# Memory-token projections set between the levels of a gated recurrence, with its value and gate rows loaded earlier

## The chip, the core and the metric

One core of one Trainium2 chip runs the whole program. The metric is the device time of the kernel in microseconds (us); the median of three runs of the kernel before is 934.94 us (934.83 to 937.43). TensorE (PE) multiplies matrices, VectorE (DVE) and ScalarE (ACT) work element by element, GpSimd (POOL) issues gathers and scatters, and SyncE (SP) issues most DMAs, in the order in which they stand in its queue. TensorE's clock has two levels, 1.2 and 2.4 GHz; the profile shows what was granted as a share of 2.4 GHz (0.50 or 1.00, or a mean over a stretch).

## The reference, cut to what matters

One decoder layer is computed for 512 prompt tokens and 8 sample tokens with the same weights. Two independent parts of it meet in this change.

```
# gated linear attention (4 heads, 64 x 128 state), exact form of S_t = diag(a_t) S_(t-1) + k_t^T v_t, o_t = q_t S_t
b    = cumsum(log_a)                                   # per chunk
attn = einsum('bhid,bhjd,bhijd->bhij', q, k, exp(b_i - b_j)), causal
o    = attn @ v + (q * exp(b)) @ S
S    = exp(b_last) * S + (k * exp(b_last - b))^T @ v
o    = rms_norm(o, gla_norm_g) * silu(r)               # r: the gate rows

# memory tokens: keys and values of 256 tokens, which nothing but the cross-attention needs
mem_k, mem_v = mem @ w_mk, mem @ w_mv                  # 256 x 1024 times 1024 x 1024, twice

# then
h = layer_norm(ALPHA * h + concat(gla_o, mla_o) @ w_out)
h = layer_norm(ALPHA * h + cross_attention(h, mem_k, mem_v))
h = layer_norm(ALPHA * h + mixture_of_experts(h))      # 32 experts, 100 MB of weights
```

## The kernel before

The program is written as streams: Python generators such as `recurrence`, `memory`, `step`, `sample`, `first`. A small planner (`Streams.run`, lines 257 to 270) keeps an estimated time of TensorE, `PE.now`, and estimated times of the other engines; each `yield x` says that the stream wants to go on when `PE.now` has reached `x` (or when a condition holds). The stream of the highest priority that is due runs next, so a yield decides what lands between two pieces of a stream. The order of the matmuls on TensorE is then exactly the order in which the planner ran the streams. The instructions of the other engines and the DMAs of SP are put in order by the framework and stand near the matmuls they belong to.

`recurrence` (line 1055) has the third priority, `step` (the 8 sample tokens' gated state, line 1252) the seventh, `sample` (their later layers, line 1445) the eighth, `memory` (line 962) the eleventh. Memory work therefore comes only where all of those wait.

The attention matrix of the recurrence is built in levels. `level(lv)` (line 1109) makes, for a block size of 128, 64, 32, 16, 8, 4, 2 and 1 tokens, one tile of decayed keys and queries: a subtraction on DVE, exponentials on ACT, four products on DVE. The levels 16 to 1 and the diagonal are the fine levels, the loop `for n in range(6)` at line 1168: each is 64 small matmuls (32 x 32 outputs, two PSUM banks of the tag `psm`), and each bank is then merged into `fine` by DVE with a mask (line 1188). Three tiles serve all levels in turn, so level 2 can be built only when the matmuls of level 16 are done, and level 1 after those of level 8.

After the fine levels come the value rows `vN` and the chunk states (lines 1205 to 1228), then the gate rows `rN` (lines 1229 to 1234), then for each of four token tiles the outputs, 8 matmuls of 128 x 128 or fewer, and the gate (lines 1235 to 1248). Value and gate rows were projected long before and put aside in DRAM (`zv`, `zr`); they come back by SP. The yields `due` (line 1210) and `came[t]` (line 1234) leave 5 us of the planner's time between a load and its use.

`memory` runs 16 groups of 24 matmuls (128 x 256 outputs, `psd<-arena_r`), two for each pair of weight blocks of 512 KB: it loads a block, ACT casts it to a high part, DVE subtracts to make a low part (`load_split`, line 373), TensorE multiplies, ACT copies the result out, and the keys are transposed and put aside as `zmk`, the values as `zmv`. `first` then runs the output projection `w_out` (16 groups of two times 12 matmuls, of which 12 read `arena_c`); it starts when `recurrence` and `attention` are done. Cross-attention follows, then the experts, whose weights `in_we` come in 192 blocks of 512 KB into whatever room the arenas have.

All instructions are recorded by helpers: a matmul is line 218, a transpose 222, an operation of DVE, ACT or POOL 199, a DMA of SP 238. Tiles of the arenas share one name, `arena_f`. An f32 matmul leaves two records in the trace, an `arena_r` matmul one.

Of the kernel before, what the change touches and what calls it, by code (L numbers as in the profile page):

```python
# [36 lines left out]
LEVELS = (16, 8, 4, 2, 1)  # L37
# [260 lines left out]
def tile_hybrid_decoder_step(ctx: ExitStack, tc: tile.TileContext, a):  # L298
    nc = tc.nc
    PE = Tensor(tc, nc.tensor)  # L300
    Q = Loads(PE, nc.sync)
# [35 lines left out]
    AF_ = Arena(fpool.tile([128, COLS_F], F32, name="arena_f"), COLS_F)  # L337
# [10 lines left out]
    def after(*names):  # L348
        return lambda: done.issuperset(names)

    def room(arena, *shape, **kw):
        got = []

        def there():
            v = arena.alloc(*shape, **kw)
            if v is not None:
                got.append(v)
            return v is not None
        if not there():
            yield there  # L360
        return got[0]
# [693 lines left out]
    def recurrence():  # L1055
# [86 lines left out]
        m[16] = level(16)  # L1142
        yield ready[64]
        for c in range(2):
# [8 lines left out]
        m[8] = level(8)  # L1153
        yield ready[32]
        for c in range(2):
# [9 lines left out]
            for g in (0, 2):  # L1165
                S.copy(A[32 * g:32 * g + 32, 8 * c:8 * c + 8, 32 * g + 32:32 * g + 64], pv[32 * g:32 * g + 32])
        m[4] = level(4)
        for n in range(6):
            if n:
                kk_ = qq_ = m[LEVELS[n - 1]]  # L1170
                yield ready[LEVELS[n - 1]]
            else:
                kk_, qq_ = kT, qT
            for c in range(2):
                ps = pm()
# [28 lines left out]
        done.add("fine")  # L1204
        yield after(*(("v", t) for t in range(4)))
        vN, rN = [], []
        for t in range(4):
            vN.append((yield from room(AF_, 512)))
            Q.dma_start(vN[t], zv[:, t * 512:t * 512 + 512])
        due = PE.now + 5.0  # L1210
        St = yield from room(AF_, 4, 2, 128)
        yield due
        pk = (pd(), pd())
# [14 lines left out]
        AF_.free(kd)  # L1228
        came = []
        for t in range(4):  # L1230
            yield after(("r", t))
            rN.append((yield from room(AF_, 512)))
            Q.dma_start(rN[t], zr[:, t * 512:t * 512 + 512])
            came.append(PE.now + 5.0)
        for t in range(4):
            on = yield from room(AF_, 512)
            yield came[t]
            pss = (pd(), pd()) if t % 2 else (pm(), pm())
# [987 lines left out]
```

## Time and profile before

| what | value |
|---|---|
| median of 3 runs | 934.94 us |
| the profiled execution's own time | 936.53 us |
| span of that execution, first to last instruction | 934.8 us |
| TensorE busy | 825.0 us, 88% |
| mean granted clock | 0.919 |
| VectorE, ScalarE, GpSimd busy | 485.1, 289.1, 85.0 us |
| mean DMA rate | 247 GB/s, 230.43 MB |

The program goes through stages that follow each other on TensorE: projections and attention to about 270 us, the levels of the recurrence to about 314 us, the states and outputs of the recurrence among memory projections to about 395 us, the output projection, the cross-attention to about 569 us, its output projection, and the experts from about 640 us. A share over the whole span therefore says little; the answers below are for single stretches. "Idle" is time in which an engine had no instruction of its own running; the name after the arrow is what ended it.

### The profile page before, as it was taken

How to read it: one execution, taken by the hardware profiler on the slowest of the kernel's cores; microseconds unless marked ns; L12 is line 12 of the kernel's file. 1: busy time of each engine (PE TensorE's matmuls, PEld its weight loads, DVE VectorE, ACT ScalarE, POOL GpSimd, SP SyncE). 2: the span in 40 equal slices, each digit the busy share in tenths (PEclk: the TensorE clock that was granted, in tenths of full speed). 3: DMA queues.
4: the chain of work that ended last, by engine and by line, in shares of the span. 5: the costliest groups of instructions: out<-in, count | busy, mean ns of one | idle time of the engine just before them, and what ended most of it. 6: DMA issues, size and time to landing. Idle time of an engine off the chain costs nothing. (4 is left out here: it accounts for less than half of the span.)

```text
span 934.8 us, 17185 instructions
## 1 busy us (share of the span) xinstructions
PE 825.0 (88%) x6767; PEld 585.0 (63%) x6767; DVE 485.1 (52%) x1079; ACT 289.1 (31%) x612; POOL 85.0 (9%) x88
## 2 busy tenths in 40 slices
PE   7999999989987899999899999995899959379991
PEld 6898566667875779989588757993344334133441
DVE  5564257683756525644762264567543644253734
ACT  4322334452542144412333241112123213122421
POOL 3100111011420000000000000001200200200101
PEclk9998999999985679999899999996989979779996
DMA  7922687667771447987847664257899999969930
GB/s 252 312 71 73 188 276 230 222 224 219 247 283 49 126 151 217 350 318 278 306 169 253 216 214 154 90 183 258 326 372 408 410 407 408 409 231 408 410 119 23
DMA packets 83961, 230.43 MB, mean 247 GB/s; under 512 B 12483, under 2 KB 32989, under 8 KB 83493
## 3 DMA queue, kind: packets, MB, share of 16 engines
q1 hardware_dynamic: 74660, 203.98, 61.2%
q0 software_dynamic: 9216, 25.31, 7.7%
q8 instruction: 55, 0.90, 0.4%
q14 instruction: 30, 0.24, 0.1%
HBM read 223.11 MB, written 14.39 MB: 254 GB/s over the span
## 5 line engine op out<-in xcount | busy, mean ns | idle before, releaser
L218 PE MATMUL psd<-arena_r 128*128 128x256 f32 (+1 forms) x2208 | 294.8, 293 | 9.5 <-ACT arena_r L199 5.4
L218 PEld LDWEIGHTS psd<-arena_r 128*128 128x128 f32 x2208 | 281.2, 198 | 24.0 <-issue 12.6
L218 PE MATMUL psx<-arena_f 96*32 96x256 f32 (+1 forms) x752 | 134.0, 491 | 2.0 <-DMA arena_f<-in_latT 2.0
L199 DVE TENSOR_TENSOR arena_r<-arena_f,arena_r 128x1024 fp32r<-128x1024 f32 (+3 forms) x71 | 82.4, 1166 | 100.9 <-ACT arena_r L199 90.3
L199 ACT CAST arena_r<-arena_f 128x1024 fp32r<-128x1024 f32 (+3 forms) x73 | 71.1, 977 | 130.3 <-PE psd L218 85.5
L218 PE MATMUL psm<-arena_f 64*32 64x32 f32 (+10 forms) x1394 | 94.6, 306 | 16.1 <-DVE arena_f L199 5.7
L218 PE MATMUL pss<-arena_f 128*8 128x256 f32 (+5 forms) x478 | 85.6, 465 | 0.7 <-ACT arena_f L199 0.7
L218 PEld LDWEIGHTS psx<-arena_f 96*32 96x32 f32 (+1 forms) x752 | 44.8, 124 | 63.6 <-issue 51.9
L218 PEld LDWEIGHTS psm<-arena_f 64*32 64x32 f32 (+6 forms) x1384 | 53.4, 145 | 49.0 <-issue 28.7
L222 PE MATMUL psm<-cst,arena_f 128*128 128x128 f32 (+2 forms) x393 | 64.0, 295 | 18.2 <-ACT arena_f L199 5.1
L199 DVE TENSOR_TENSOR arena_f<-arena_f 128x1024 f32<-128x1024 f32 (+6 forms) x72 | 57.1, 827 | 37.8 <-DMA arena_f<-h2d,arena_s 33.3
L222 PEld LDWEIGHTS psm<-cst,arena_f 128*128 128x128 f32 (+2 forms) x393 | 47.6, 156 | 41.8 <-issue 18.4
L637 POOL DMA_INDIRECT arena_f<-in_latN,ixn x32 | 34.0, 1063 | 192.1 <-PE psm L218 176.9
L199 DVE SCALAR_TENSOR_TENSOR arena_f<-arena_f,psd 128x256 f32<-128x256 f32 (+2 forms) x60 | 28.8, 488 | 41.6 <-PE psd L218 32.1
L1843 POOL DMA_INDIRECT arena_f<-h2d,arena_s x24 | 24.8, 1035 | 238.6 <-PE psm L222 139.3
L218 PEld LDWEIGHTS pss<-arena_f 128*8 128x8 f32 (+3 forms) x468 | 28.0, 120 | 24.8 <-issue 14.7
L199 DVE SCALAR_TENSOR_TENSOR arena_m<-pss,arena_s,arena_m 128x512 fp32r<-128x512 f32 x32 | 24.0, 749 | 31.7 <-ACT arena_m L199 31.7
L218 PE MATMUL psx<-arena_l,arena_f 128*64 128x512 f32 x100 | 39.9, 592 | 0.0
L222 PE MATMUL pss<-cst,arena_f 128*128 128x128 f32 x32 | 7.7, 326 | 36.1 <-DVE arena_m L199 25.8
L199 DVE TENSOR_TENSOR arena_f<-arena_f,psx 128x256 f32<-128x256 f32 x16 | 6.7, 417 | 61.0 <-ACT arena_f L199 61.0
L199 ACT ACTIVATE arena_f<-psd 128x256 f32<-128x256 f32 (+3 forms) x55 | 19.9, 363 | 53.6 <-PE psd L218 43.8
L199 ACT ACTIVATE arena_f<-psx 128x256 f32<-128x256 f32 x16 | 6.1, 384 | 97.1 <-PE psx L218 91.9
(210 smaller groups left out, 945.7 us busy)
## 6 DMA issues: line engine op xcount, KB each, us to landing
arena_f<-in_we SPq DMA_DIRECT2D x129, 512.0 KB
arena_l<-in_we SPq DMA_DIRECT2D x40, 512.0 KB
arena_f<-in_latT SPq DMA_DIRECT2D x128, 144.0 KB
arena_d<-in_we SPq DMA_DIRECT2D x23, 512.0 KB
arena_f<-in_wout SPq DMA_DIRECT2D x16, 512.0 KB
arena_f<-in_memKT SPq DMA_DIRECT2D x16, 512.0 KB
arena_f<-in_wxq SPq DMA_DIRECT2D x16, 512.0 KB
arena_f<-in_memV SPq DMA_DIRECT2D x16, 512.0 KB
```

Source lines behind the costliest of these rows:

```text
L199: return f(out, *args, **kw)
L218: return self.queue(self.eng.matmul(out, lhsT, rhs, **kw))
L222: return self.queue(self.eng.transpose(out, src, ident))
L637: G.indirect_dma_start(out=out, out_offset=None, in_=src, in_offset=bass.IndirectOffsetOnAxis(ap=ix, axis=0))
L1843: G.indirect_dma_start(out=out, out_offset=None, in_=h2d, in_offset=bass.IndirectOffsetOnAxis(ap=ix, axis=0), bounds_check=NT - 1, oob_is_ ...
```

## The change

Four things change, all in `recurrence`. Ahead of level 64, of level 32 and of each fine level the yield now asks for 1 us of the planner's time beyond `PE.now` (or for the level's readiness, if later), so that a stream of lower priority gets a turn there. The loads of the four value tiles and the four gate tiles are issued together, in front of the fine levels, once both have been projected. The yields of 5 us between these loads and their use are gone; 0.5 us stand in their place, and one yield until DVE and ACT are nearly through. Nothing that is computed changes, and no instruction is added but by the planner's different order.

```
@@ -1140,7 +1140,7 @@
         m[16] = level(16)
-        yield ready[64]
+        yield max(ready[64], PE.now + 1.0)
@@ -1151,7 +1151,7 @@
         m[8] = level(8)
-        yield ready[32]
+        yield max(ready[32], PE.now + 1.0)
@@ -1165,12 +1165,20 @@
         m[4] = level(4)
+        yield after(*((z, t) for z in "vr" for t in range(4)))
+        vN, rN = [], []
+        for z, vs in ((zv, vN), (zr, rN)):
+            for t in range(4):
+                vs.append((yield from room(AF_, 512)))
+                Q.dma_start(vs[t], z[:, t * 512:t * 512 + 512])
         for n in range(6):
             if n:
                 kk_ = qq_ = m[LEVELS[n - 1]]
-                yield ready[LEVELS[n - 1]]
+                yield max(ready[LEVELS[n - 1]], PE.now + 1.0)
             else:
                 kk_, qq_ = kT, qT
+                yield PE.now + 1.0
@@ -1202,14 +1210,8 @@
         done.add("fine")
-        yield after(*(("v", t) for t in range(4)))
-        vN, rN = [], []
-        for t in range(4):
-            vN.append((yield from room(AF_, 512)))
-            Q.dma_start(vN[t], zv[:, t * 512:t * 512 + 512])
-        due = PE.now + 5.0
         St = yield from room(AF_, 4, 2, 128)
-        yield due
+        yield PE.now + 0.5
         pk = (pd(), pd())
@@ -1226,15 +1228,10 @@
         AF_.free(kd)
-        came = []
-        for t in range(4):
-            yield after(("r", t))
-            rN.append((yield from room(AF_, 512)))
-            Q.dma_start(rN[t], zr[:, t * 512:t * 512 + 512])
-            came.append(PE.now + 5.0)
+        yield PE.ready() - 0.5
         for t in range(4):
             on = yield from room(AF_, 512)
-            yield came[t]
+            yield PE.now + 0.5
```

On TensorE, from the sample tokens' state matmuls (64x256) to the chunk states (64x128), the kernel before has these rows in this order; 32x32 are the levels (32 matmuls of level 32, then six fine levels of 64), 32x256 is paged attention, `arena_r` 128x256 is a memory projection:

```order
L218 MATMUL psm<-arena_f 64x256 x8
L218 MATMUL psm<-arena_f 32x32 x96
L218 MATMUL psm<-arena_f 32x256 x16
L218 MATMUL psm<-arena_f 32x32 x128
L222 MATMUL psm<-cst,arena_f 128x128 x2
L218 MATMUL psm<-arena_f 32x32 x192
L218 MATMUL psm<-arena_f 64x256 x8
L218 MATMUL psd<-arena_r 128x256 x48
L218 MATMUL psd<-arena_f 64x128 x16
```

The changed kernel has, from the same place (the first 32x32 row is level 32), and up to the third fine level:

```order
L218 MATMUL psm<-arena_f 32x32 x32
L218 MATMUL psm<-arena_f 32x256 x16
L218 MATMUL psm<-arena_f 64x256 x8
L222 MATMUL psm<-cst,arena_f 128x128 x2
L218 MATMUL psd<-arena_r 128x256 x24
L218 MATMUL psm<-arena_f 32x32 x64
L218 MATMUL psm<-arena_f 32x128 x16
L218 MATMUL psd<-arena_r 128x256 x24
L218 MATMUL psm<-arena_f 32x32 x64
L222 MATMUL psm<-cst,arena_f 128x128 x4
L218 MATMUL psd<-arena_r 128x256 x24
```

The pattern goes on in that way: six projections of 24 lie ahead of the last fine level where none lay before, one in front of each fine level, and parts of `step` lie there too.

The outputs of the recurrence are the 128x128 rows of line 218 (those of line 222 are transposes). On TensorE before they stand in a row after one projection:

```order
L218 MATMUL psd<-arena_r 128x256 x24
L218 MATMUL psm<-arena_f 128x128 x4
L218 MATMUL psd<-arena_f 128x128 x8
L218 MATMUL psm<-arena_f 128x128 x8
L218 MATMUL psd<-arena_f 128x128 x8
L218 MATMUL psm<-arena_s,ones 128x32
```

In the changed kernel the same four groups, with a projection or a piece of `sample` (8x256) between each two:

```order
L218 MATMUL psm<-arena_f 128x128 x4
L218 MATMUL psd<-arena_r 128x256 x24
L222 MATMUL psd<-cst,arena_f 128x128 x4
L218 MATMUL psd<-arena_f 128x128 x8
L218 MATMUL psm<-arena_f,arena_s 8x256 x8
L218 MATMUL psm<-arena_f 128x128 x8
L218 MATMUL psd<-arena_r 128x256 x24
L222 MATMUL psd<-cst,arena_f 128x128 x4
L218 MATMUL psd<-arena_f 128x128 x8
```

All 16 memory projections still come ahead of the first row of `w_out`, as before; more of `sample` comes ahead of it than before.

On SP, just after the last load of paged keys, as a piece of the difference:

```order
+L238 DMA arena_f<-in_wmk 128x1024 x2
 L238 DMA arena_f<-in_cst 8x512
 L238 DMA arena_f<-in_memT 128x1024 x2
-L238 DMA arena_f<-in_wmk 128x1024 x2
-L238 DMA arena_f<-zv 128x512
-L238 DMA arena_f<-zr 128x512 x3
+L238 DMA arena_f<-zv 128x512 x4
+L238 DMA arena_f<-zr 128x512 x4
 L238 DMA arena_f<-in_wmk 128x1024 x5
```

Eight loads of value and gate rows instead of four now stand ahead of five blocks of memory weights; the other four stood behind these.

## Rows read from the trace of the kernel before

**Rows 1.** The page: TensorE's share, and its clock in 40 equal slices of the span.
```profile
PE 825.0 (88%) x6767; PEld 585.0 (63%) x6767; DVE 485.1 (52%) x1079; ACT 289.1 (31%) x612; POOL 85.0 (9%) x88
...
PEclk9998999999985679999899999996989979779996
```

**Rows 2.** Busy time by stretch: stretch, its length, busy us (instructions) of each engine.
```profile
core 0: us, PE busy (x) PEld busy (x) DVE busy (x) ACT busy (x) POOL busy (x), PEclk, DMA share, GB/s
...
285.00:314.00 29.00, 21.45 (x883) 15.75 (x880) 17.81 (x43) 7.35 (x13) 0.00 (x0) 0.56 0.19 58
314.00:336.00 22.00, 22.00 (x192) 20.58 (x192) 8.84 (x19) 8.79 (x21) 0.00 (x0) 0.88 0.56 172
336.00:355.00 19.00, 17.48 (x67) 13.68 (x66) 6.72 (x26) 5.04 (x29) 0.00 (x0) 0.55 0.36 127
355.00:395.00 40.00, 39.46 (x372) 36.67 (x371) 21.44 (x31) 19.23 (x29) 0.00 (x0) 1.00 0.89 289
395.00:456.00 61.00, 59.91 (x613) 53.88 (x616) 30.09 (x63) 13.48 (x25) 0.00 (x0) 1.00 0.83 301
...
640.00:895.00 255.00, 214.08 (x1031) 93.66 (x1032) 121.04 (x245) 66.59 (x136) 33.25 (x30) 0.90 0.95 369
```

**Rows 3.** TensorE in order of time, the levels: start, us, line, operands, records, idle before.
```profile
284.85 3.68 PE L218 MATMUL psm<-arena_f 64*32 64x32 f32 x166 [2.11 <-DVE arena_f L199]
289.75 6.74 PE L218 MATMUL psm<-arena_f 64*32 64x32 f32 x256 [1.23 <-issue]
298.39 0.71 PE L218 MATMUL psm<-arena_f 64*32 64x32 f32 x58 [1.90 <-issue]
...
306.04 1.92 PE L218 MATMUL psm<-arena_f 64*32 64x32 f32 x127 [1.02 <-issue]
309.32 4.67 PE L218 MATMUL psm<-arena_f 64*32 64x32 f32 x78 [1.36 <-issue]
313.93 8.43 PE L218 MATMUL psd<-arena_r 128*128 128x256 f32 x48
```

**Rows 4.** TensorE in order of time, the recurrence's outputs and projections behind them.
```profile
332.82 3.30 PE L218 MATMUL psd<-arena_f 128*128 128x128 f32 x16
337.64 5.86 PE L218 MATMUL psm<-arena_f 128*128 128x128 f32 x16 [1.52 <-DVE arena_f L199]
343.43 5.86 PE L218 MATMUL psd<-arena_f 128*128 128x128 f32 x16
...
350.30 4.58 PE L218 MATMUL psd<-arena_r 128*128 128x256 f32 x24
...
365.03 5.99 PE L218 MATMUL psd<-arena_r 128*128 128x256 f32 x48
```

**Rows 5.** Groups of TensorE instructions by shape, 285 to 314 us: busy, mean ns, idle before.
```profile
L218 PE MATMUL psm<-arena_f 64*32 64x32 f32 x832 | 13.9, 232 | 9.7 <-issue 5.5 <-DVE arena_f L199 2.7 <-DVE arena_s L199 1.4
```

**Rows 6.** Groups of ACT and DVE instructions by shape, 260 to 395 us.
```profile
L199 ACT CAST arena_r<-arena_f 128x1024 fp32r<-128x1024 f32 x20 | 20.8, 1047 | 21.6 <-PE psd L218 12.8 <-DMA arena_f<-in_wmk 8.8
...
L199 DVE TENSOR_TENSOR arena_r<-arena_f,arena_r 128x1024 fp32r<-128x1024 f32 x20 | 24.4, 1223 | 30.3 <-ACT arena_r L199 28.0 <-PE psd L218 1.8 <-DMA out_mem_k<-arena_f 0.5
```

**Rows 7.** In order of time, a weight's cast on ACT, and TensorE behind it.
```profile
277.48 1.04 ACT L199 CAST arena_r<-arena_f 128x1024 fp32r<-128x1024 f32 x1 [6.70 <-DMA arena_f<-in_wmk]
278.43 0.57 ACT L199 COPY arena_f<-psm 64x512 f32<-64x512 f32 x1
...
279.06 3.68 PE L218 MATMUL psm<-arena_f 8*64 8x256 f32 x16 [2.29 <-ACT arena_f L199]
```

**Rows 8.** TensorE in order of time: the first group of the output projection.
```profile
394.94 1.57 PE L218 MATMUL psd<-arena_r,arena_c 128*128 128x256 f32 x12
```

**Rows 9.** TensorE's waits among the experts, 640 to 935 us: total, times, longest.
```profile
PE pss L222 <- DVE arena_m L199: 25.8, 2, 20.9
PE pss L222 <- DVE arena_f L199: 10.3, 1, 10.3
```

## The prediction, made before the changed kernel ran

> **What bounds the kernel now.** I read the page first: TensorE is busy 88% of the span and its clock is at full nearly everywhere but in a dent of the 13th to 15th slice [rows 1]. A change that only moves TensorE's work can gain in such dents alone, so I then read the busy time by stretch [rows 2]. From 314 to 336 and from 355 to 456 us TensorE has hardly a gap and runs at 1.00. The dents are 285 to 314 us, where it works 21.45 of 29 us at a clock of 0.56, and 336 to 355 us, 17.48 of 19 us at 0.55. TensorE in order of time names them: the first is the fine levels, small matmuls with waits of 1 to 2 us in front of most groups [rows 3]; the second is the outputs of the recurrence [rows 4]. In the first, the 9.7 us of idle ahead of the level matmuls (those between 285 and 314 and the one that ends at 284.85) is put down to DVE and to TensorE's own queue [rows 5], that is, a level waits for the merge and the building of levels. DVE itself works 17.81 of these 29 us, ACT 7.35 [rows 2], so neither is full: the stretch is bound by the latency of a chain that hops between three engines. The last row by which the two kernels can be compared is the first group of the output projection at 394.94 us [rows 8]: all 16 memory projections and the whole recurrence lie ahead of it in both.
>
> **What the change removes.** Since TensorE does the same work, the gain ahead of that row is idle removed plus time given back by the clock.
>
> Idle: 29.00 - 21.45 = 7.55 us in the levels and 19.00 - 17.48 = 1.52 us in the outputs [rows 2], 9.1 us in all. Six projections now lie ahead of the last fine level. At full clock one takes half of 5.99 us, 3.0 us [rows 4], longer than any of the waits [rows 3], so they can cover all of it.
>
> Clock: the two projections at 313.93 take 8.43 us where two at full clock take 5.99, so 2.4 us are lost there [rows 3, 4]. Two pieces of the outputs of the recurrence take 5.86 us each where a piece of as many records took 3.30, so 5.1 us [rows 4]. The projection at 350.30 takes 4.58 instead of 3.0, so 1.6 us. Together 9.1 us.
>
> The small level matmuls, 13.9 us in all [rows 5], may gain from the clock as well; between nothing and a half, 7 us. The nearest rows are two level groups: 58 records in 0.71 us at 298.39, 12.2 ns each, against 127 in 1.92 us, 15.1 ns each [rows 3]. If all others came to the pace of the better, 19% of 13.9 us, 2.6 us, would be saved; I take that.
>
> Gross: 9.1 + 9.1 + 2.6 = 20.8 us.
>
> **What it adds.** (a) The first projection between levels starts at about 294 us, when the clock has not yet risen, and it will run as the first of the two at 313.93 did: 2.4 us, between 0 and 2.4.
>
> (b) Not every wait goes. Each weight block brings a cast of 1.05 us on ACT and a subtraction of 1.22 us on DVE [rows 6], and these now stand in the queues between the exponentials, products and merges of the levels. Six such subtractions add 7.3 us to DVE's 17.8 [rows 2]; 25 us lie beside TensorE's 13.9 of levels and 6 x 3.0 of projections, 32 us and more with the paged attention and the step, so DVE does not become the bound, but some merges will come late. The cost lies between 0 and the 9.7 us that were waited before [rows 5]; I take 3.0, about two waits of the sizes that stand there now [rows 3].
>
> (c) The loads of 256 KB for value and gate rows cost nothing where they are used (DMA is busy 19% from 285 to 314 us, and the stretch after it has no gap [rows 2]). But eight instead of four now stand on SP ahead of five blocks of memory weights, and one of these ends a wait of 6.70 us of ACT; behind that cast stands a copy for which TensorE waits 2.29 us [rows 7]. One more MB takes, at the 369 GB/s of the experts' stretch, which is 95% busy, some 2.7 us. Cost 0 to 2.7; I take 0.5, because the loads are issued some 20 us before that cast.
>
> (d) The weights of memory and sample, the residual rows and the outputs crowd into less time. By the order on SP about 24 MB are issued from the last level to the first row of the output projection, in some 75 us, 320 GB/s; the stretch from 355 to 395 us had 289 GB/s at a share of 0.89 with TensorE idle for 0.5 us, and 369 at 0.95 is the most that a long stretch shows [rows 2]. Cost 0 to 5; I take 3.0.
>
> (e) The experts' blocks. The order on SP with its waits shows that from the 21st block on each waits for the matmul for which the block after it waited before: the arena's room is cut differently and holds one block less. One block of 0.52 MB at 369/0.95 GB/s is 1.35 us, paid once if DMA is the bound there, as 0.95 says [rows 2]. Cost 0 to 1.4; I take 1.4.
>
> The rest moves without a price. The pieces of `sample` that come earlier than the output projection are taken from its fillers later. From 395 us on TensorE has 1.1 us of idle up to 456 [rows 2] and the same stages follow in the same order, so what is gained at 394.94 is carried to the end.
>
> Net: 20.8 - 2.4 - 3.0 - 0.5 - 3.0 - 1.4 = 10.5 us. The profiled execution took 936.53 us and would take 926.0; the median of the runs, 934.94, becomes 924.4 us. About 0.3%, 2.8 us, is what a measurement here can tell from no change.
>
> **The skill against the trace.** ACT takes its instructions in order in rows 7: the copy waits behind a cast that waits for DMA. The Trainium skill, page "TensorE: Matmul & The Clock Gate", section "Architectural detail: the array is 16× 32×32, not 1× 128×128", states that ScalarE and VectorE are strict FIFOs; the trace agrees, by the 2.29 us, and rival 2 is what that rule would do here. In rows 4 TensorE runs at half pace from 337.64 through 349 without a gap between the two groups. The same page, section "What's actually happening", says that the clock is throttled by default and activity releases the throttle; here 11.7 us of work did not release it, so for this kind of matmul the trace differs, and by the page alone the clock would be no rival once the gaps are filled.
>
> **The rivals.** 1. The clock stays low or falls again between levels. For it: the levels themselves ran through 6.74 us without a gap and the stretch still has 0.56 [rows 2, 3], and the outputs above. Against it: the projections at 313.93 brought it up within their 8.43 us [rows 3]. If all six projections in the levels ran at the slow pace, the other five would cost 5 x 2.4 = 12 us more, and the 2.6 of the levels be lost; but slower projections cover the waits (3.0) and thin out the loads (some 2). Net 10.5 - 12 - 2.6 + 5 = 1 us, half of it 6 us: 928 to 934, centre 931.
>
> 2. The queues hold the levels up. Each cast between levels waits for a block's buffer or its DMA, and the exponentials stand behind it. At 2.29 us [rows 7] for each of six casts, 13.7 us instead of the 3.0 that I took: the net is 10.5 - 10.7, no change, 935. For it: rows 7. Against it: all blocks but one of these were asked for before the levels start, when DMA is nearly free [rows 2].
>
> 3. The gain is larger: no late merges (b), no crowding (d), the levels at half of their 13.9 us. 10.5 + 6.0 + 4.4 = 21 us: 914.
>
> 4. Slower: the experts turn on the missing block. TensorE already waits 25.8 and 10.3 us there for DVE work that stands behind gathers [rows 9]. If the missing block were paid not once but at each of the 16 pairs of experts, 15 x 1.35 = 20 us would be added: 924 + 20 = 944. From the ninth further pair on it outweighs the gain. For it: the loads fill room as it is freed. Against it: at 0.95 busy, DMA has only 13 of 255 us to lose [rows 2].
>
> That the change doesn't do what it says can be left out: the order on TensorE shows the projections between the levels.
>
> **How the numbers follow.** My forecast 53%, 918 to 929; rival 1 24%; rival 2 8%; rival 3 9%; rival 4 6%. Predicted is the forecast's 924.4. The range leaves out rival 4, most of rival 2 and the better half of rival 3: 911 to 933. Faster by over 0.3% (below 932.1): 53 + 9 + four fifths of 24 = 81, and 2 of rival 2, 83%. Within 0.3%: 5 + 5 = 10%. Slower: 6 + 1 = 7%.
>
> **What would show it.** In the changed kernel's profile: the first group of the output projection at 383 to 389 us (12 us earlier, less the pieces of `sample` that now come ahead of it); the clock of 285 to 314 above 0.8 and no half-pace group among the outputs; less than 4 us of idle from 285 to 336; the experts' stretch as long as before within 3 us. A clock near 0.6 in the levels would make rival 1 right, waits put down to ACT or DVE of over 10 us in them rival 2, and a longer experts' stretch rival 4. The sum is wrong if the first group of the output projection comes there and the end doesn't follow it.

## The result, and the profile after

The changed kernel takes 925.99 us (median of 20 runs, 920.48 to 934.53) where the kernel before, run beside it, took 935.59 (20 runs). The ratio is 0.9891, with a 95% interval of 0.9867 to 0.9915. One of the 20 runs, 934.53 us, counts as slow and is left out of the ratio. The prediction was 924.4 us, 911 to 933. The size was right; by which steps it came about is another matter.

| what | before | after |
|---|---|---|
| profiled execution, its own time | 936.53 us | 928.61 us |
| its span | 934.8 us | 926.7 us |
| TensorE busy | 825.0 us | 818.6 us |
| mean granted clock | 0.919 | 0.932 |
| level 64 starts (TensorE, 64x64) | 274.07 us | 274.25 us |
| first chunk state (TensorE, 64x128) | 322.29 us | 331.55 us |
| first group of the output projection | 394.94 us | 393.28 us |

The page after, TensorE's share and its clock in 40 slices (before: [rows 1]):

```profile
PE 818.6 (88%) x6767; PEld 580.2 (63%) x6767; DVE 486.7 (53%) x1079; ACT 295.0 (32%) x616; POOL 85.7 (9%) x88
...
PEclk9998999999996998999899999997999979789996
```

The three slices of 5, 6 and 7 tenths in the first half have become one of 6. Busy time by stretch after (before: [rows 2], cut there at 395; columns as there):

```profile
core 0: us, PE busy (x) PEld busy (x) DVE busy (x) ACT busy (x) POOL busy (x), PEclk, DMA share, GB/s
285.00:314.00 29.00, 27.06 (x573) 21.65 (x568) 16.50 (x36) 6.71 (x13) 0.00 (x0) 0.80 0.48 148
314.00:336.00 22.00, 19.96 (x549) 18.32 (x549) 14.21 (x30) 11.93 (x16) 0.00 (x0) 0.92 0.68 212
336.00:355.00 19.00, 16.38 (x123) 13.35 (x122) 7.84 (x22) 8.67 (x26) 0.00 (x0) 0.91 0.75 268
355.00:383.00 28.00, 25.94 (x214) 22.38 (x214) 15.88 (x35) 12.04 (x34) 0.00 (x0) 0.88 0.61 209
```

From 285 to 314 us TensorE is idle for 1.94 us instead of 7.55, at a clock of 0.80 instead of 0.56. But behind that the stretches from 314 to 395 us had 2.1 us of idle before, and the three from 314 to 383 us have 6.7 us now, and none of them runs at 1.00. The idle was less removed than moved.

TensorE in order of time after, levels first (before: [rows 3]) and then the outputs (before: [rows 4]): start, us, operands, records, idle before.

```profile
292.61 4.81 PE L218 MATMUL psd<-arena_r 128*128 128x256 f32 x24
...
301.32 0.42 PE L218 MATMUL psm<-arena_f 128*32 128x128 f32 x5 [1.57 <-issue]
301.67 3.14 PE L218 MATMUL psd<-arena_r 128*128 128x256 f32 x24
304.73 1.31 PE L218 MATMUL psm<-arena_f 64*32 64x32 f32 x128
...
318.08 0.76 PE L218 MATMUL psm<-arena_f 64*32 64x32 f32 x64 [1.97 <-DVE arena_f L199]
318.83 1.12 PE L218 MATMUL psm<-arena_s,arena_f 128*64 128x8 f32 x32
319.88 4.63 PE L218 MATMUL psd<-arena_r 128*128 128x256 f32 x24
...
344.37 1.22 PE L218 MATMUL psm<-arena_f 128*128 128x128 f32 x4 [2.38 <-DVE arena_f L199]
345.25 4.18 PE L218 MATMUL psd<-arena_r 128*128 128x256 f32 x24
...
349.70 3.30 PE L218 MATMUL psd<-arena_f 128*128 128x128 f32 x16
...
356.94 2.26 PE L218 MATMUL psm<-arena_f 128*128 128x128 f32 x8 [1.29 <-DVE arena_f L199]
359.14 5.49 PE L218 MATMUL psd<-arena_r 128*128 128x256 f32 x24
...
365.01 3.30 PE L218 MATMUL psd<-arena_f 128*128 128x128 f32 x16
```

A fine level of 128 records takes 1.31 us here, 10.2 ns each, where one took 1.92, 15.1 ns each. Between the levels stand projections of 3.14 us. Four projections, at 292.61, 319.88, 345.25 and 359.14, take 4.2 to 5.5 us instead. The first comes while the clock is still low from the stretch ahead of it (granted 0.50 from 283.06 to 292.27 us); each of the others stands behind a wait for DVE of 1.29 to 2.38 us, with at most 2.3 us of work between. What DVE does there matters for the outputs: at 344.37 and 356.94 TensorE waits for banks of PSUM out of which DVE still reads a piece of `sample`. On DVE, in order of time:

```profile
343.00 1.32 DVE L199 TENSOR_TENSOR arena_f<-arena_f,psm 8x256 f32<-8x256 f32 x3
...
355.57 1.32 DVE L199 TENSOR_TENSOR arena_f<-arena_f,psm 8x256 f32<-8x256 f32 x3
```

The same work can be put side by side. From the start of level 64 to the first group of the output projection TensorE's groups by shape are, before and then after (busy us, mean ns, idle ahead of them):

```profile
L218 PE MATMUL psd<-arena_r 128*128 128x256 f32 x384 | 52.5, 299 | 0.5 <-DVE arena_r L199 0.5
L218 PE MATMUL psm<-arena_f 64*32 64x32 f32 x832 | 13.9, 232 | 9.7 <-issue 5.5 <-DVE arena_f L199 2.7 <-DVE arena_s L199 1.4
L218 PE MATMUL psd<-arena_f 128*128 128x128 f32 x16 | 5.0, 407 | 0.0
L218 PE MATMUL psm<-arena_f 128*128 128x128 f32 x16 | 4.2, 388 | 1.5 <-DVE arena_f L199 1.5
```

```profile
L218 PE MATMUL psd<-arena_r 128*128 128x256 f32 x384 | 56.4, 310 | 1.0 <-DVE arena_f L199 1.0
L218 PE MATMUL psm<-arena_f 64*32 64x32 f32 x832 | 10.2, 199 | 4.1 <-DVE arena_f L199 4.1
L218 PE MATMUL psm<-arena_f 128*128 128x128 f32 x16 | 4.1, 370 | 3.7 <-DVE arena_f L199 3.7
L218 PE MATMUL psd<-arena_f 128*128 128x128 f32 x16 | 3.7, 313 | 0.0
```

So in this stage: idle ahead of levels 9.7 to 4.1; levels 13.9 to 10.2; all outputs with the terms that read the chunk states `St` (the two rows above, and two of 64 partitions, 5.1 to 3.9 and 3.2 to 2.2) 17.5 to 13.9; but the 16 projections 52.5 to 56.4, and the idle ahead of outputs 1.5 to 3.7. The sum is 5.6 + 3.7 + 3.6 - 3.9 - 2.2 = 6.8 us. The stage itself went from 120.87 to 119.03 us, 1.8 shorter, with 4.9 us more of `sample` in it (rows of 3.4, 1.0 and 0.5 us): 6.7 us, which agrees; rows that are not listed change by up to 2.0 us each and nearly cancel.

### The profile page after: what moved, and what is told of

Its sections match the earlier page's. It is cut to its first block, busy times and chain, and to the rows that moved or that the text cites. A ratio compares the mean times of both kernels' runs of the same rounds, so it can differ in the third digit from the quotient of the medians.

```text
span 926.7 us, 17162 instructions
## 1 busy us (share of the span) xinstructions
PE 818.6 (88%) x6767; PEld 580.2 (63%) x6767; DVE 486.7 (53%) x1079; ACT 295.0 (32%) x616; POOL 85.7 (9%) x88
## 5 line engine op out<-in xcount | busy, mean ns | idle before, releaser
L218 PE MATMUL psd<-arena_r 128*128 128x256 f32 (+1 forms) x2208 | 298.0, 295 | 7.8 <-ACT arena_r L199 5.5
L218 PEld LDWEIGHTS psd<-arena_r 128*128 128x128 f32 x2208 | 283.9, 200 | 20.3 <-issue 8.5
L218 PE MATMUL psx<-arena_f 96*32 96x256 f32 (+1 forms) x728 | 126.1, 492 | 3.3 <-DMA arena_f<-in_latT 3.1
L218 PE MATMUL psm<-arena_f 64*32 64x32 f32 (+10 forms) x1394 | 89.6, 285 | 13.0 <-DVE arena_f L199 9.3
L218 PE MATMUL pss<-arena_f 128*8 128x256 f32 (+5 forms) x466 | 91.3, 468 | 1.7 <-DMA arena_f<-in_memV 1.0
L222 PE MATMUL psm<-cst,arena_f 128*128 128x128 f32 (+2 forms) x393 | 62.0, 287 | 18.9 <-DVE arena_f L199 4.5
L218 PEld LDWEIGHTS psx<-arena_f 96*32 96x32 f32 (+1 forms) x728 | 42.6, 124 | 57.1 <-issue 43.5
L218 PEld LDWEIGHTS psm<-arena_f 64*32 64x32 f32 (+6 forms) x1384 | 48.9, 123 | 45.7 <-issue 24.2
L222 PEld LDWEIGHTS psm<-cst,arena_f 128*128 128x128 f32 (+2 forms) x393 | 45.7, 152 | 43.4 <-issue 20.8
L218 PE MATMUL pss<-arena_l,arena_f 128*64 128x512 f32 x92 | 42.9, 608 | 0.0
L222 PE MATMUL pss<-cst,arena_f 128*128 128x128 f32 x32 | 7.7, 326 | 37.4 <-DVE arena_m L199 27.3
## 6 DMA issues: line engine op xcount, KB each, us to landing
arena_l<-in_we SPq DMA_DIRECT2D x46, 512.0 KB, 10.8
```

Source lines behind the costliest of these rows:

```text
L218: return self.queue(self.eng.matmul(out, lhsT, rhs, **kw))
L222: return self.queue(self.eng.transpose(out, src, ident))
```

## The experiments

Each kernel's ratio is to the kernel before, run on the same chip beside it, with a 95% interval. Single profiles are compared only from level 64 on: ahead of it TensorE's order is the same in all, yet the start of level 64 lies between 273.33 and 282.14 us in the profiled executions. Behind it they scatter too: f2, whose order on TensorE up to the experts is that of the kernel before, takes 653.6 us from level 64 to the end of its profiled execution, the kernel before 660.7, and 4.8 us of that lie among the experts (279.1 and 283.9). So a gain or loss of a few us is told by the ratios, and the profiles tell where the time goes.

The theory was that the projections between levels carry the gain, through idle and clock. The rivals were that the early loads and short waits carry it, or that `sample` work pulled ahead does. In the table, outputs in a "row" follow each other; "apart" means that a yield stands in front of each.

| kernel | level yields | loads | waits behind them | outputs | median us | ratio, interval |
|---|---|---|---|---|---|---|
| changed kernel | yes | in front of level n = 0 | 0.5 us | apart | 925.99 | 0.9891, 0.9867 to 0.9915 |
| e1 | yes | as before | 5 us | row | 922.64 | 0.9873, 0.9824 to 0.9922 |
| e2 | no | in front of n = 0 | 0.5 us | apart | 939.69 | 1.0052, 1.0020 to 1.0083 |
| e3 | yes | in front of n = 0 | 0.5 us | row | 932.06 | 0.9971, 0.9943 to 1.0000 |
| e4 | changed kernel, four expert blocks less | | | | 927.51 | 0.9900, 0.9865 to 0.9935 |
| e5 | yes | in front of n = 0 | 5 us | row | 929.14 | 0.9933, 0.9898 to 0.9968 |
| e6 | yes | as before | 5 us | apart | 923.46 | 0.9863, 0.9822 to 0.9905 |
| e7 | no | in front of n = 0 | 5 us | row | 943.54 | 1.0056, 1.0023 to 1.0090 |
| e8 | yes, 2.5 us | as before | 5 us | row | 927.57 | 0.9890, 0.9840 to 0.9940 |
| f1 | yes | in front of n = 3 | 0.5 us | apart | 925.25 | 0.9892, 0.9852 to 0.9931 |
| f2 | no | in front of n = 3 | 5 us | row | 935.18 | 0.9981, 0.9954 to 1.0009 |
| f3 | no, but eight rooms asked for | as before | 5 us | row | 940.43 | 1.0054, 1.0030 to 1.0078 |
| f4 | yes | in front of n = 3 | 5 us | row | 925.97 | 0.9918, 0.9890 to 0.9946 |

**e1, the yields of the levels alone** (against the kernel before; the same in front of levels 64 and 32):

```diff
+                yield max(ready[LEVELS[n - 1]], PE.now + 1.0)
-                yield ready[LEVELS[n - 1]]
...
+                yield PE.now + 1.0
```

> The kernel before with the yields of the levels alone: projections come between the levels, while value and gate rows are loaded where they were and the 5 us between these loads and their use stay, so the four outputs of the recurrence stand together in a row. In the profiled runs of before and after, the level matmuls lost 3.7 us of busy time (13.9 to 10.2) and 5.6 us of idle (9.7 to 4.1), and 9.6 us of the median were gained. Theory A (the projections between the levels carry the gain): 929 to 931 us, more than half of the gain, with the level matmuls at 10 to 11 us of busy time, and a clock near 0.5 left in the stretch of the outputs. Rival B (the early loads and the short waits behind them carry it): 934 to 937 us, no change. If the parts add up, this and the next kernel together gain about 9.6 us.

Measured: 922.64 us, ratio 0.9873, better than the 929 to 931 of theory A: the yields alone give the whole gain. TensorE's groups from level 64 to the output projection show the levels nearly as in the changed kernel, and in order of time the outputs, which stand in a row, run at full pace without a wait:

```profile
L218 PE MATMUL psm<-arena_f 64*32 64x32 f32 x832 | 11.2, 207 | 3.9 <-DVE arena_f L199 3.2 <-issue 0.6
```

```profile
342.85 1.05 PE L218 MATMUL psm<-arena_f 128*128 128x128 f32 x8
343.74 3.30 PE L218 MATMUL psd<-arena_f 128*128 128x128 f32 x16
346.97 3.40 PE L218 MATMUL psm<-arena_f 128*128 128x128 f32 x16
350.31 3.40 PE L218 MATMUL psd<-arena_f 128*128 128x128 f32 x16
```

A dent of the clock at the outputs, which I had expected here, is not there: the granted clock is 1.00 from 342.85 to 353.6 us. From level 64 to the first group of the output projection this execution takes 111.6 us where the kernel before takes 120.9, with some 3 us more of `sample` in it. So the gain lies in this stage, which speaks against the rival that `sample` work pulled ahead makes it; that rival has no run of its own.

**e2, all but the yields of the levels** (against the changed kernel, each yield of the levels as before):

```diff
-                yield max(ready[LEVELS[n - 1]], PE.now + 1.0)
+                yield ready[LEVELS[n - 1]]
...
-                yield PE.now + 1.0
```

> The changed kernel with the yields of the levels as before: value and gate rows are loaded in front of the fine levels and the short yields stand, so projections separate the outputs of the recurrence, but the six fine levels stand in a row without a projection. Theory A (levels carry more than half): 930 to 933 us, the dent of the clock in the levels back (about 0.56) and the level matmuls at 13 to 14 us busy with 8 to 10 us of idle ahead of them; what is gained, 3 to 5 us, comes from the outputs. Rival B: 925 to 927 us, all of the gain.

Measured: 939.69 us, slower than before, outside of both expectations. The rival falls: early loads and short waits bring nothing by themselves. But theory A had 3 to 5 us of gain here and there is a loss, so something in this half of the change costs.

**e3, the outputs in a row** (against the changed kernel):

```diff
             on = yield from room(AF_, 512)
-            yield PE.now + 0.5
```

> The changed kernel without the yield of 0.5 us in front of each output tile: levels are separated by projections as in the changed kernel, the four outputs of the recurrence stand in a row. The prediction put 5.1 us on the half pace of such a row. Theory A (a row of them runs at the low clock): 928 to 931 us, 2 to 5 us slower than the changed kernel, with a stretch of output matmuls at about 366 ns each. Rival C (once the clock is up in front of them it stays up, and the row costs nothing): 925 to 927 us, outputs at about 206 ns each.

Measured: 932.06 us, 6.1 us slower than the changed kernel, just above the range of this run's theory A, and the intervals do not touch. In order of time:

```profile
345.52 5.86 PE L218 MATMUL psm<-arena_f 128*128 128x128 f32 x16 [1.20 <-DVE arena_f L199]
351.30 5.86 PE L218 MATMUL psd<-arena_f 128*128 128x128 f32 x16
...
358.91 4.36 PE L218 MATMUL psd<-arena_r 128*128 128x256 f32 x24
```

That is the picture of [rows 4]: a wait of 1.2 us for DVE, and then 11.7 us at half pace. In this setting a row of outputs does run at the low clock, and rival C falls. Together with e1 it points to what decides: not that the outputs stand in a row, but that TensorE waits at their head.

**e4, room for four expert blocks less** (against the changed kernel):

```diff
+            if len(spare) < 4 and len(parts) <= 180:
+                spare.append(v)
+                continue
             e, u = parts.pop(0)
```

> The changed kernel with room for four more weight blocks of 0.52 MB taken away from the experts for good (four pieces of the arena are taken when the 13th block has been asked for, and never used). The prediction put 1.35 us, once, on each missing block: then 4 x 1.35 = 5.4 us slower than the changed kernel, about 931 us. Rival D (the number of blocks in flight is not what bounds the experts): 925 to 927 us. Rival 4 of the prediction (a missing block is paid at every pair of experts): 20 us for each block, 980 us and more.

Measured: 927.51 us; its ratio is 0.0009 above that of the changed kernel, 0.8 us, give or take 4. Rival 4 is out, by a factor of ten and more. The 5.4 us that my price gave lies just outside, and the trace does not show it either: from the first matmul of the experts to the end this kernel takes 930.1 - 645.86 = 284.2 us, the changed one 926.7 - 641.32 = 285.4, a difference within the scatter named above. Rival D stands.

**e5, the 5 us put back, loads in front** (against the changed kernel; 5 us ahead of the states, once 5 us ahead of the outputs):

```diff
+        due = PE.now + 5.0
...
-        yield PE.now + 0.5
+        yield due
...
-        yield PE.ready() - 0.5
+        came = PE.now + 5.0
...
-            yield PE.now + 0.5
+            yield came
```

> The changed kernel with the 5 us of the kernel before put back ahead of the chunk states and once ahead of the outputs, in place of the 0.5 us; the loads of value and gate rows stay in front of the fine levels. It differs from the first run of these experiments (the yields of the levels alone, 922.6 us) in the place of the loads alone, and from the changed kernel (926.0 us) in the waits alone. Theory E (the short waits cost: an output tile comes up before DVE is done, TensorE waits and its clock falls): 921 to 924 us, the outputs at 206 to 213 ns each without a wait ahead of them. Rival F (the loads in front cost, by what they push back on SP or by the room they take): 925 to 928 us.

Measured: 929.14 us, outside theory E's range and just above that of rival F. It is the yields alone with the loads in front, and is 6.5 us slower than these by the medians, though the intervals overlap. Longer waits did not cure it: a group of outputs again stands behind a wait of 1.16 us, its 16 records take 4.55 us, and the next 16 take 5.86 at half pace.

What TensorE waits for there can be followed. It needs a bank of PSUM out of which DVE reads the first outputs; DVE needs the root of their squares from ACT; and ACT first loads a table of functions, 1.28 us. ACT, DVE and TensorE of e5, in order of time:

```profile
349.48 1.28 ACT L199 ACT_TABLE_LOAD   x1
350.77 0.30 ACT L199 ACTIVATE rs<-ss,eps_r 128x4 f32<-128x4 f32 x1
...
351.10 0.18 DVE L199 RECIPROCAL rs<-rs 128x4 f32<-128x4 f32 x1 [1.71 <-ACT rs L199]
351.32 1.13 DVE L199 SCALAR_TENSOR_TENSOR arena_f<-psm,rs,arena_f 128x128 f32<-128x128 f32 x4
...
352.24 4.55 PE L218 MATMUL psm<-arena_f 128*128 128x128 f32 x16 [1.16 <-DVE arena_f L199]
```

The kernel before (at 334.88 us) and e3 (342.76) load a table at this place too, and TensorE waits 1.52 and 1.20 us behind it. In e1, e8 and f4, whose outputs stand in a row and run at full pace, ACT goes from the squares to the root without a load:

```profile
345.18 0.23 ACT L199 ACTIVATION_READ_ACCUMULATOR arena_f<-psm 128x1 f32 x1
345.44 0.30 ACT L199 ACTIVATE rs<-ss,eps_r 128x4 f32<-128x4 f32 x1
```

That is e1, where the one load of this stage stands at 315.77 us, for the root that `step` takes behind the last exponentials of the levels. In e5, e3 and the changed kernel this root comes ahead of the last exponentials, so the tables are changed three times (in the changed kernel at 316.26, 319.10 and 346.28 us). No run moves a table load alone; that it makes the wait is read from these traces, not tested.

**e6, the yields of the levels, and outputs apart** (against e1):

```diff
-            yield came[t]
+            yield max(came[t], PE.now + 0.5)
```

> The kernel before with the yields of the levels and, behind the 5 us that stay, 0.5 us in front of each output tile, so that projections also separate the outputs; loads as in the kernel before. Against the first run of these experiments (922.6 us) the separation of the outputs is the only difference. Where the outputs stand in a row there they already ran at 206 to 213 ns each, full pace. Theory E: nothing left to gain, 921 to 925 us. Rival G (the separation is worth what it was worth in the changed kernel, 932.1 - 926.0 = 6 us): 916 to 918 us.

Measured: 923.46 us, as e1. Separating the outputs is worth 6 us in the changed kernel and nothing here: the number is theory E's, and rival G falls. It also fits the table load, which stands among the outputs in the changed kernel and not here. But not all outputs run at full pace in the profiled execution (927.25 us): a piece of `sample` between them waits 2.55 us for DVE, and the 16 records behind it take 5.86 us.

**e7, the early loads alone** (against the kernel before; the loads of lines 1205 to 1209 and 1230 to 1233 go away, and 5 us stand once ahead of the outputs):

```diff
         m[4] = level(4)
+        yield after(*((z, t) for z in "vr" for t in range(4)))
+        vN, rN = [], []
+        for z, vs in ((zv, vN), (zr, rN)):
+            for t in range(4):
+                vs.append((yield from room(AF_, 512)))
+                Q.dma_start(vs[t], z[:, t * 512:t * 512 + 512])
```

> The kernel before with the loads of value and gate rows in front of the fine levels and nothing else: the yields of the levels and all waits of 5 us stand as before. Theory E: the loads cost nothing by themselves, 934 to 937 us, as before (935.6 to 936.4). Rival F (the loads cost what the second run lost, 939.7 - 936.4 = 3.3 us): 938 to 941 us.

Measured: 943.54 us, ratio 1.0056 (2 to 8 us by its interval), the median above both expectations. I had the loads down as nearly free; by the ratio they cost about 5 us by themselves. The order on TensorE says where to look. As a difference from the kernel before, in the levels:

```
 L218 MATMUL psm<-arena_f 64x256 x8
-L218 MATMUL psm<-arena_f 32x32 x96
+L218 MATMUL psm<-arena_f 32x32 x32
 L218 MATMUL psm<-arena_f 32x256 x16
-L218 MATMUL psm<-arena_f 32x32 x128
-L222 MATMUL psm<-cst,arena_f 128x128 x2
-L218 MATMUL psm<-arena_f 32x32 x192
 L218 MATMUL psm<-arena_f 64x256 x8
+L222 MATMUL psm<-cst,arena_f 128x128 x2
+L218 MATMUL psm<-arena_f 32x32 x384
```

The work that stood between the levels now stands ahead of the first. The program says why. Each load first asks the arena for 512 columns (`room`), and by the planner's own account 80 columns are free at that place. So the recurrence stands there until others give columns back, and streams of lower priority use up, in that wait, what they would have done between the levels.

**e8, level yields of 2.5 us** (against e1):

```diff
-                yield max(ready[LEVELS[n - 1]], PE.now + 1.0)
+                yield max(ready[LEVELS[n - 1]], PE.now + 2.5)
```

> The first kernel of these experiments with 2.5 us of the planner's time in the yields of the levels where 1.0 stood. One projection still stands ahead of each fine level from the second on; the difference is in front, where level 32 and the first fine level stand in a row and a half of the sample tokens' state matmuls comes ahead of them. Theory A with its price of idle: what counts is that each level finds its merge done; with the same number of projections between levels 920 to 925 us. A rival H (each us of waiting in the planner is paid, since work of lower priority is taken from places where it covers waits later): 926 to 930 us.

Measured: 927.57 us, 0.9890. By its median this is rival H, but the interval holds e1 as well. It decides nothing.

**f1, f2, f3: is it the wait for room or the transfer?** At the fourth fine level (n = 3) there is room. f1 is the changed kernel, f2 the kernel before, each with the eight loads there:

```diff
         for n in range(6):
...
+            if n == 3:
+                vN, rN = [], []
+                for z, vs in ((zv, vN), (zr, rN)):
+                    for t in range(4):
+                        vs.append((yield from room(AF_, 512)))
+                        Q.dma_start(vs[t], z[:, t * 512:t * 512 + 512])
```

f3 is the kernel before, loads where they were, with only the asking for room in front of the levels:

```diff
         m[4] = level(4)
+        got = []
+        for t in range(8):
+            got.append((yield from room(AF_, 512)))
+        AF_.free(got)
```

> The changed kernel with the eight loads of value and gate rows issued in front of the fourth fine level instead of the first. At the first one the arena has 80 free columns and the recurrence stands until 512 and more are given back; at the fourth there is room and it does not stand. Yields of the levels, short waits and separated outputs are those of the changed kernel. Theory R (the loads in front cost because the recurrence waits for room there, and what would have stood between the levels is used up in that wait): 920 to 923 us, 3 to 6 us faster than the changed kernel and like the yields alone (922.6 us). Rival F (early loads cost by the transfers or the room that they hold): 925 to 928 us.

> The kernel before with the eight loads issued in front of the fourth fine level and all else as before; TensorE's order up to the experts is that of the kernel before. On SP the loads stand in the same place as in the run with the early loads alone but for two blocks of memory weights. Theory R (the transfers and the held room cost nothing, the wait for room does): 934 to 937 us, as before. Rival F: 939 to 944 us, as the run with the early loads alone (943.5 us).

> The kernel before with the wait for room alone: in front of the fine levels eight pieces of 512 columns are asked for and given back at once, and the loads stay where they were. TensorE's order in the levels is that of the run with the early loads alone: 64x256 of the sample tokens ahead of all six fine levels, which stand in a row. Theory R: 939 to 944 us, 3 to 8 us slower than before. Rival F: 934 to 937 us, as before.

Measured: f2 935.18 us, ratio 0.9981: early loads that need not wait cost nothing. f3 940.43 us, ratio 1.0054: the wait without any load moved costs what e7 cost. The intervals of f2 and f3 do not touch. In the kernel without level yields this decides for theory R, for loads in front of the fourth level. The levels of f3 from level 64 to the output projection:

```profile
L218 PE MATMUL psm<-arena_f 64*32 64x32 f32 x832 | 13.9, 240 | 13.7 <-issue 10.2 <-DVE arena_f L199 2.8 <-DVE arena_s L199 0.6
```

13.7 us of idle where the kernel before has 9.7. In e2 and e7 it is 13.7 and 13.1, in f2 10.5. That these 4.0 us make up the cost is not shown: the profiled execution was the fastest of f3's twelve (935.51 us), takes 2.1 us more than the kernel before from level 64 to the output projection (123.0 and 120.9), and no more to the end (660.3 and 660.7). The 5 us stand on the ratios.

f1 came out at 925.25 us, 0.9892, in the range of rival F: no faster than the changed kernel, where theory R had 920 to 923. With projections between the levels the wait for room shows no cost in this pair. What f1's trace shows is where separate outputs and short waits can lead; a piece of `sample` waits for the bank of the first outputs, and the outputs behind it run at half pace:

```profile
336.96 1.88 PE L218 MATMUL psm<-arena_f,arena_s 128*8 128x256 f32 x16 [2.31 <-DVE arena_f L199]
338.77 5.86 PE L218 MATMUL psd<-arena_f 128*128 128x128 f32 x16
344.56 4.32 PE L218 MATMUL psd<-arena_r 128*128 128x256 f32 x24
```

**f4, f1 with 5 us in place of the short waits** (edit as in e5):

> The kernel of the run with the loads in front of the fourth fine level, with 5 us ahead of the chunk states and once ahead of the outputs in place of the short waits; so the yields of the levels, early loads without a wait for room, and the outputs in a row behind projections. TensorE's order up to the outputs is that of the yields alone but for one piece of the sample tokens. Theory E (the short waits cost: in the run with the loads in front of the fourth level TensorE waited 2.31 us for DVE among the outputs and 16 of their records took 5.86 us): 920 to 923 us, the outputs at full pace without a wait ahead. Rival F (early loads hold room and cost, whatever the waits): 925 to 928 us. Between the two lies what the spread of the runs can't tell apart, 923 to 925 us.

Measured: 925.97 us, ratio 0.9918. The outputs do run at full pace (3.30, 3.40 and 3.40 us for 16 records), as theory E had it, but the time is rival F's, and E's 920 to 923 us lie below the interval (923.6 to 928.8). F's price is not shown by that: the intervals of f4, f1 and e1 overlap.

## Why the prediction was right, and where it was not

**The idle of the levels (gain 7.55) and the late merges (cost 3.0): held.** The idle ahead of the level matmuls fell from 9.7 to 4.1 us; 5.6 us of net gain where the two steps had about 4.6. Counted by stretch it is less, 7.55 to 3.98 from 285 to 336 us, mostly because the wait of 1.57 us at 301.32 stands ahead of a piece of `step`. One merge came late as foreseen: at 318.08 us TensorE waits 1.97 us, and on DVE a weight's subtraction of 1.23 us and level products of 1.43 us stand ahead of that merge.

**The level matmuls (2.6): held, a little small.** They lost 3.7 us.

**The clock (gain 9.1, cost 2.4 for the first projection): failed.** Of 5.1 us at the outputs 3.6 came. The projections were to gain 2.4 + 1.6 and lose 2.4, and instead lost 3.9 us. Step (a) priced one slow projection. There are four, over the 3.1 us of a fast one by 1.7, 1.5, 1.0 and 2.4 us, 6.6 together, where the kernel before loses the 4.0 that were to be gained. I had counted waits as idle and the clock as a separate thing; three of the four stand behind a wait for DVE. That is rival 1 in part, and the sign that no group among the outputs would run at half pace failed too (granted clock 0.50 at 344.37).

**The idle of the outputs (gain 1.52): wrong sign.** It rose from 1.5 to 3.7 us. The prediction let the pieces of `sample` move without a price, but the two waits, 2.38 and 1.29 us, are for banks from which DVE still reads such pieces, the first of them late, behind two subtractions of weights (1.23 and 1.21 us). The wait that the kernel before has in its row, behind a table load, is covered in the changed kernel by the projections that separate the outputs: without them the kernel is 6 us slower (e3).

**(c) the loads (0.5, at most 2.7): the wrong mechanism.** I priced transfers and places on SP, and where f2 measures them, in front of the fourth level, they are free. What costs is that the recurrence waits for room in front of the levels, and that was to be read from the order: in the kernel before this wait alone makes 5 us (f3). Whether it costs in the changed kernel, between its projections, stays open: e5 against e1 says 6.5 us, the changed kernel against f1 says nothing, f4 and f1 lie in the range of rival F, and the intervals overlap.

**(d) crowding (3.0): not seen.** Up to 395 us DMA ends no wait of TensorE among the larger ones; the longest that it ends from there to 560 us is 1.0 us.

**(e) one expert block (1.4): not so.** The experts' stage did grow by 1.5 us (283.9 to 285.4), but four blocks less did not lengthen it further (e4), and 1.5 us lie within what single executions scatter there (f2: 279.1). In the profile they are TensorE's long waits for DVE, 27.3 and 10.1 us after, 25.8 and 10.3 before [rows 9].

**The sum.** At the output projection the steps gave 20.8 - 2.4 - 3.0 - 0.5 - 3.0 = 11.9 us, and 6.7 came. The sum is right as a sum; its terms are not. The first group was to stand at 383 to 389 us and stands at 393.28, with 4.9 us more of `sample` ahead of it. From there to the end another 1.6 us came, 8.3 from level 64 on, against 10.5; the medians differ by 9.6. As the experts took 1.5 us more, 3.0 us came between the output projection and the experts, where nothing was priced. That the total was hit is therefore luck in good part: the clock was about 7 us too high (5.5 for the projections, 1.5 for the outputs) and the idle of the outputs 3.7, and against these stood crowding (3.0) and loads (0.5) that cost nothing, levels that gave 2.1 more, and those 3.0. Of the signs, the idle from 285 to 336 us (3.98 us, under 4) and the experts' stage (within 3 us) held, the clock of 285 to 314 came out at its limit (0.80), and the place of the first output-projection group and the pace of the outputs failed. The mechanism of the gain, projections between levels, is right and shown by e1 and e2: the changed kernel with and without the level yields lies 15 us apart (0.9891 and 1.0052).

**The rivals.** Rival 2 (queues hold the levels) is seen once, 1.97 us, not six times. Rival 3 fell. Rival 4 fell by e4; by its own numbers it would outweigh the gain from the eighth further pair on (8 x 1.35 = 10.8 us), not the ninth. "Slower" had a mechanism that I did not list: the wait for room.

**Better than both?** The yields alone (e1) and with the outputs apart (e6) have the lowest medians, 922.64 and 923.46 us. They are faster than the kernel before; from the changed kernel the runs do not tell them apart. The four lines of the level yields do the work.

## What to carry to other kernels

A chain that hops between engines can be filled with pieces of independent work, one between each two hops: here, with pieces of 3.1 us and waits of 1 to 2 us, that was worth 12 to 15 us, from idle and from the clock. Before an allocation is moved ahead of such a chain, look at what is free there: a stream that waits for room lets its fillers run too early, and the transfer, which looks like the cost, was free here. A wait of 1 to 2 us on TensorE is often not paid once; price the work behind it at the low pace too. And follow such a wait to its source before choosing a cure: in e5 the engine named, DVE, was itself waiting for a table load on ACT, which the longer waits did not take away.

## What the runs showed of the hardware

How far a short wait reaches was not expected. In e3 a wait of 1.20 us is followed by 11.7 us at half pace without a gap (granted clock 0.50); in f1 one of 2.31 us by 5.86 us for 16 records that take 3.30 elsewhere. But not each wait does it: after 1.57 us at 301.32 in the changed kernel the next projection took 3.14 us, full pace. The Trainium skill, page "TensorE: Matmul & The Clock Gate", section "HAM oscillation — how this bites in real kernels", describes a loop, with longer waits than these, whose every tile starts at the low clock because TensorE waited in front of it; e3 and f1 show the same behind 1.20 and 2.31 us, the row at 301.32 does not. A wait alone does not tell the pace behind it.

The way back differed from row to row. A projection (`arena_r`) that starts slow is through in 4.2 to 5.5 us and the next one takes 3.1, as at 301.67. The outputs (`arena_f`, 128x128) stayed at half pace for their whole 11.7 us in e3, without a gap, and the projection behind them was the first to run faster (4.36 us where a slow one took up to 5.49 us, granted 0.67). It is not the type f32 alone: in the kernel before the clock came up amid the small level matmuls (0.50 to 295 us, 0.80 from 295.0 to 296.4). No run separates type, shape and place.
